# One written order for the start of a streaming-encoder kernel: a root for each row tile, the norm weight spread by one-row matmuls, queries projected beside keys and values

## The chip, the core and the metric

The kernel runs on one NeuronCore of a Trainium2 chip. Its engines work side by side, each through its own list of instructions in order: TensorE (PE in the profile; PEld is its weight load), VectorE (DVE), ScalarE (ACT), GpSimd (POOL) and SyncE (SP), which here issues the loads and most of the stores. They wait for one another by semaphores. The metric is the device time of one execution in microseconds, from three runs.

## The reference

```python
h = rmsnorm(x, norm_g)                    # x: 2048 prompt rows, then 64 sample rows, 1024 wide
q, k, v, ga, u, gb, mg = split(h @ w_in)  # w_in: 1024 x 7168
att = stick_breaking(q, k, v)             # 8 heads of 128; no softmax
pb  = multi_scale_pool(u) @ w_pool * pool_scale
m   = sigmoid(mg_a) * ((att * silu(ga)) @ w_br_a) + sigmoid(mg_b) * ((pb * silu(gb)) @ w_br_b)
y   = rmsnorm(x + m @ w_out, final_g)

def rmsnorm(x, g):
    return x * rsqrt(mean(x * x, axis=-1) + 1e-6) * g
```

Prompt and sample rows go through the same layer (the sample rows with a cache of 4096 keys and values). Keys and values are outputs too. All is fp32. A product of two matrices is made of three products of rounded fp32 halves: each operand is split into a rounded "hi" and the remainder "lo", and hi·hi, lo·hi and hi·lo are added up.

## The kernel before

**Halves and tiles.** The rows are worked in two halves: the first holds 1024 prompt rows and the 64 sample rows, nine row tiles of 128 rows (tile 8 has 64), the second the other 1024. For a half, the normalised rows are kept transposed as `hhi` and `hlo` (128 partitions, 8 blocks of the model width, all rows). From them the kernel projects slab by slab; a slab is 128 columns of `w_in`: a head's keys, values, queries or gate. `proj` (L276) loads a slab's weights in two halves of 512 columns a partition (`raw`), splits them into `whi` (ACT, L81) and `wlo` (L82, on POOL for the first head of a half), and runs 24 products for each group of rows (L284 to L286: hi·hi, lo·hi, hi·lo for 8 blocks) into a PSUM bank `pj`.

**From x to hhi.** A row tile comes as two halves of 512 columns (b = 0, 1). `square_sum` (L177) squares a half on ACT and adds it up into a column of `ss`; `root` (L87 to L93) turns the columns of several tiles at once into `rstd`, with a square root on ACT and a Newton step in tiny DVE instructions; `normalise` multiplies by `rstd` and by the norm weight `g_bc` (L204 on DVE for b = 0; for b = 1 from tile 2 on, L201 on DVE and L202 on POOL). `g_bc` are two tiles of 128 x 512 into which a DMA copies the weight for each partition (L194). `transposed_h` turns a half on PE in four transposes (L211) into a PSUM bank `tr`, of which there are two; ACT copies it to `hhi` (L81) and DVE writes the remainder to `hlo` (L82).

**The first half's start.** `prepare_x0` takes tiles 0 and 1 (loads, squares, one root, normalise), `build_h0` transposes them; then come tiles 2 and 3, 4 and 5, and 6 to 8, each set under one root. In head 0 keys and values are projected in "fine" groups of 256, 256, 256 and 320 rows, two slabs at a time, so that each group needs only two more tiles; the queries follow in groups of 512, 256 and 320, then the gate.

**The second half's start.** `build_h1` is called for tiles 0 to 3 and for 4 to 7: each time the weight is copied again by `norm_gain`, and each half tile `xb` is loaded, normalised and transposed beside the last gate slabs of the first half and the first fine slabs of the second. `g_bc` and `xb` share eight buffers (tag `be`).

**What sets the order.** PE's instructions stand as the Python code emits them; `run` interleaves generators by estimated times. The order on ACT, DVE, POOL and SP is made by the framework's scheduler, and each engine then runs its list strictly in order.

Of the kernel before, what the change touches and what calls it, by code (L numbers as in the profile page):

```python
# [11 lines left out]
ALU = mybir.AluOpType  # L12
# [32 lines left out]
def kernel(  # L45
# [4 lines left out]
    y_prompt, y_sample, k_prompt, v_prompt, pool_prompt, k_sample, v_sample, pool_sample,  # L50
):
    nc = tc.nc

    xp, xs = x_prompt[0], x_sample[0]
    yp, ys = y_prompt[0], y_sample[0]
# [20 lines left out]
    def split(hi, lo, src, eng=None):  # L76

        if eng == "v":
            nc.vector.tensor_copy(hi, src)
        else:  # L80
            nc.scalar.copy(hi, src)  # L81
        (nc.gpsimd if eng == "g" else nc.vector).tensor_tensor(lo, src, hi.bitcast(F32), op=ALU.subtract)  # L82
# [62 lines left out]
    with ExitStack() as front:  # L145
# [7 lines left out]
        def stage(name):  # L153
            return side.tile([P, 528], F32, name=name, tag="st", bufs=4)
# [27 lines left out]
        def root(c0, n):  # L182
            rsqrt_of_mean(rstd[:, c0:c0 + n], ss[:, c0:c0 + n], [t[:, c0:c0 + n] for t in sq])

        def load_x(half, i, b, t):
            src, m = row_tile(half, i)
            nc.sync.dma_start(t[0:m, 0:512], src[:, b * 512:(b + 1) * 512])
            return m

        def norm_gain():  # L190
            g = []
            for b in range(2):
                g.append(attp.tile([P, 528], F32, name="g_bc", tag="be", bufs=8))
                nc.sync.dma_start(g[b][:, 0:512], norm_g[0:1, b * 512:(b + 1) * 512].broadcast_to([P, 512]))  # L194
            return g

        def normalise(half, i, b, m, xt, gain):
            c = half * 9 + i
            x = xt[0:m, 0:512]
            if b and c > 1:  # L200
                nc.vector.tensor_scalar(x, x, rstd[0:m, c:c + 1], None, op0=ALU.mult)  # L201
                nc.gpsimd.tensor_tensor(x, x, gain[b][0:m, 0:512], op=ALU.mult)  # L202
            else:
                nc.vector.scalar_tensor_tensor(x, x, rstd[0:m, c:c + 1], gain[b][0:m, 0:512],  # L204
                                               op0=ALU.mult, op1=ALU.mult)

        def transposed_h(i, b, m, xt):
            tr = psum.tile([P, 512], F32, name="tr")
            trv = tr.rearrange("p (j r) -> p j r", j=4)
            for j in range(4):  # L210
                nc.tensor.transpose(trv[:, j, 0:m], xt[0:m, j * P:(j + 1) * P], ident[0:m, 0:m])  # L211
            split(hhi[:, b * 4:b * 4 + 4, i * P:i * P + m], hlo[:, b * 4:b * 4 + 4, i * P:i * P + m],
                  trv[:, :, 0:m])
            return 436.0

        x0 = {}
        gain0 = []

        def prepare_x0(i0, i1):
            for i in range(i0, i1):  # L220
                m = DEC if i == 8 else P
                if 4 <= i < 8:
                    both = attp.tile([P, 2, 512], F32, name="xt2", tag="v", bufs=4)
                for b in range(2):
                    if i < 4:
                        xt = attp.tile([P, 512], F32, name="xt", tag=("khi", "klo")[b], bufs=4)
                    elif i < 8:
                        xt = both[:, b]
                    else:
                        xt = stage("xt")  # L230
                    load_x(0, i, b, xt)
                    square_sum(i, b, m, xt)
                    x0[i, b] = xt
            if not gain0:
                gain0.extend(norm_gain())
            root(i0, i1 - i0)
            for i in range(i0, i1):
                for b in range(2):
                    normalise(0, i, b, DEC if i == 8 else P, x0[i, b], gain0)

        def build_h0(i0, i1):
            for i in range(i0, i1):
                for b in range(2):
                    yield transposed_h(i, b, DEC if i == 8 else P, x0[i, b])

        def stats1():
            for i in range(8):
# [13 lines left out]
                    normalise(1, i, b, P, xt, gain)  # L261
                    yield transposed_h(i, b, P, xt)

        def load_w(src, kts, width, eng=None):

            whi = pool.tile([P, kts, width], F32R, name="whi", tag="whi", bufs=2)
            wlo = pool.tile([P, kts, width], F32R, name="wlo", tag="wlo", bufs=2)
            sv = src.rearrange("(k p) c -> p k c", p=P)
            step = 512 // width
            for k in range(0, kts, step):  # L270
                raw = pool.tile([P, step, width], F32, name="raw", tag="raw", bufs=3)
                nc.sync.dma_start(raw, sv[:, k:k + step, :])
                split(whi[:, k:k + step], wlo[:, k:k + step], raw, eng)
            return whi, wlo

        def proj(groups, slabs, eng=None):  # L276


            ws = [load_w(win[:, col:col + P], KT, P, eng) for col, _ in slabs]
            for g, (c0, n) in enumerate(groups):  # L280
                for (whi, wlo), (_, evac) in zip(ws, slabs):
                    ps = psum.tile([P, 512], F32, name="pj")
                    for k in range(KT):
                        nc.tensor.matmul(ps[:, 0:n], whi[:, k], hhi[:, k, c0:c0 + n], start=k == 0, stop=False)  # L284
                        nc.tensor.matmul(ps[:, 0:n], whi[:, k], hlo[:, k, c0:c0 + n], start=False, stop=False)  # L285
                        nc.tensor.matmul(ps[:, 0:n], wlo[:, k], hhi[:, k, c0:c0 + n], start=False, stop=k == KT - 1)  # L286
# [180 lines left out]
        def head_proj(half, hd, fine=False):  # L467
# [86 lines left out]
            yield from proj(groups, [(OFF_Q + col, evac_q)])  # L554
            yield from proj(groups, [(OFF_GA + col, evac_g)])
            heads[half, hd] = out

# [281 lines left out]
        fine_ns = 2 * 24 * mm_ns(256)  # L839


        first = head_proj(0, 0, True)
# [153 lines left out]
    E = mybir.EngineType  # L996
    bpsum = ctx.enter_context(tc.tile_pool(name="bpsum", bufs=2, space=PSUM))
    ahead = {}

# [430 lines left out]
```

## Time and profile before

| | us |
|---|---|
| median of 3 runs | 2761.02 (2757.12 to 2761.07) |
| the profiled execution | 2762.22 |
| its span, first to last instruction | 2760.5 |
| granted PE clock, mean | 0.996 |
| ACT busy | 1267.9 (46%) |
| POOL busy | 583.5 (21%) |
| bytes moved by DMA | 343.87 MB, 125 GB/s |

How to read it: a row of the timeline has the start, the duration, the engine, the line of the kernel, the instruction and its tiles (`out<-in`), and in square brackets how long the engine had been idle and what ended that. A row of the waits has the waiting instruction, what ended the wait, the total in us, the number of waits and the longest. A row of the groups has the count, the busy time in us and the mean in ns. A matmul's record is longer than the distance to the next one, since matmuls are pipelined; the distance is what counts.

### The profile page before, as it was taken

The numbers are of one execution on the slowest core, as the hardware profiler recorded it, in microseconds if no ns is written. First come the engines' busy times: TensorE is split into PE (matmuls) and PEld (weight loads), VectorE is DVE, ScalarE is ACT, GpSimd is POOL, SyncE is SP. The second block draws the span as 40 slices with busy tenths as digits, with TensorE's granted clock in tenths as the row PEclk, the third lists the DMA queues.
The fourth block names the chain that finished last, engine by engine and source line by source line (L and its number), as shares of the span: only waits on it lengthen the run. The fifth ranks groups of instructions, "written<-read, shape, count | busy, mean of one in ns | idle before, by whom it ended". The sixth has DMA issues, their size and how long they took to land.

```text
span 2760.5 us, 41803 instructions
## 1 busy us (share of the span) xinstructions
PE 2702.0 (98%) x15052; PEld 2361.2 (86%) x15052; DVE 1835.7 (66%) x2843; ACT 1267.9 (46%) x2520; POOL 583.5 (21%) x1285
## 2 busy tenths in 40 slices
PE   6999999999999999999999999999999999999998
PEld 6988888888898989888888888887778889999886
DVE  6555555567777784487888888786453236777876
ACT  4445444455555553355555655564222223333443
POOL 2112222220000001322433342342004601111001
PEclk9999999999999999999999999999999999999999
DMA  5224222224444445311111111112336757786753
GB/s 149 77 83 131 75 72 72 76 94 152 150 154 153 148 147 158 97 43 58 54 45 52 50 50 43 54 46 81 106 98 218 261 176 265 257 288 224 246 160 119
DMA packets 344397, 343.87 MB, mean 125 GB/s; under 512 B 30062, under 2 KB 286558, under 8 KB 344188
## 3 DMA queue, kind: packets, MB, share of 16 engines
q1 hardware_dynamic: 329756, 294.26, 34.2%
q0 software_dynamic: 14432, 46.93, 4.8%
q8 instruction: 118, 1.93, 0.3%
q14 instruction: 91, 0.75, 0.1%
HBM read 232.46 MB, written 108.65 MB: 124 GB/s over the span
## 4 chain that ended last, share of the span: by engine, by line
PE 85%; issue 5%; DVE 5%; DMA 2%; ACT 1%; POOL 1%; SPq 0%; POOLq 0%; DVEq 0%; ACTq 0%
PE pj L284 17%; PE pj L285 17%; PE pj L286 17%; PE tr L638 4%; PE att L655 2%; PE att L654 2%; PE att L653 2%; PE z L627 2%; PE z L626 2%; PE z L625 2%; PE x L989 2%; PE x L991 2%; PE x L993 2%; PE y L989 1%; PE y L993 1%
## 5 line engine op out<-in xcount | busy, mean ns | idle before, releaser
L284 PE MATMUL pj<-hhi,whi 128*128 128x512 f32 (+2 forms) x2608 | 945.8, 363 | 0.0
L286 PE MATMUL pj<-hhi,wlo 128*128 128x512 f32 (+2 forms) x2608 | 918.2, 352 | 0.0
L285 PE MATMUL pj<-hlo,whi 128*128 128x512 f32 (+2 forms) x2608 | 917.3, 352 | 0.1
L286 PEld LDWEIGHTS pj<-hhi,wlo 128*128 128x128 f32 x2608 | 492.2, 189 | 65.1
L284 PEld LDWEIGHTS pj<-hhi,whi 128*128 128x128 f32 x2608 | 494.7, 190 | 59.5 <-ACT hhi L81 0.2
L285 PEld LDWEIGHTS pj<-hlo,whi 128*128 128x128 f32 x2608 | 493.8, 189 | 59.1 <-DVE hlo L82 0.4
L579 DVE TENSOR_TENSOR_SCAN om<-om 128x513 f32<-128x513 f32 (+3 forms) x356 | 387.7, 1089 | 212.0 <-POOL om L561 108.5
L569 ACT ACTIVATE om<-z 128x512 f32<-128x512 f32 (+2 forms) x320 | 171.6, 536 | 322.0 <-PE z L627 272.4
L82 DVE TENSOR_TENSOR wlo<-raw,whi 128x512 fp32r<-128x512 f32 x248 | 178.2, 722 | 196.6 <-ACT whi L81 195.5
L581 POOL COPY carry<-om 128x1 f32<-128x1 f32 x356 | 78.6, 221 | 918.6 <-DVE om L579 878.1
L582 DVE TENSOR_TENSOR be<-be,om 128x512 f32<-128x512 f32 (+3 forms) x356 | 230.4, 647 | 31.5
L81 ACT CAST whi<-raw 128x512 fp32r<-128x512 f32 x256 | 158.5, 624 | 182.3 <-PE pj L285 166.5
L81 ACT CAST a<-tr 128x512 fp32r<-128x512 f32 (+2 forms) x356 | 187.9, 528 | 100.6 <-PE tr L638 89.9
L82 DVE TENSOR_TENSOR a<-tr,a 128x512 fp32r<-128x512 f32 (+2 forms) x356 | 215.6, 606 | 23.9 <-ACT a L81 21.8
L638 PE MATMUL tr<-ident,be 128*128 128x128 f32 x1088 | 175.7, 274 | 6.1 <-DVE be L582 3.7
L638 PEld LDWEIGHTS tr<-ident,be 128*128 128x128 f32 x1088 | 136.1, 140 | 44.9 <-DVE be L582 8.3
L570 ACT ACTIVATE be<-z 128x512 f32<-128x512 f32 (+2 forms) x320 | 169.9, 531 | 0.0
L653 PE MATMUL att<-a,v 128*128 128x512 f32 (+1 forms) x320 | 133.2, 416 | 0.0
L574 POOL COPY om<-carry 128x1 f32<-128x1 f32 x224 | 124.1, 554 | 2.7 <-DVE be L582 0.7
L561 POOL TENSOR_SCALAR_AFFINE_SELECT om<-om 128x128 f32<-128x128 f32 x128 | 50.6, 396 | 346.1 <-ACT om L569 346.0
L655 PE MATMUL att<-a,v 128*128 128x512 f32 (+1 forms) x320 | 118.5, 370 | 3.7 <-DVE a L82 3.3
L654 PE MATMUL att<-a,v 128*128 128x512 f32 (+1 forms) x320 | 117.4, 367 | 0.0
(316 smaller groups left out, 4677.6 us busy)
## 6 DMA issues: line engine op xcount, KB each, us to landing
raw<-in_w_in_dram SPq DMA_DIRECT2D x256, 256.0 KB, 3.1
sg<-sm_d SPq DMA_DIRECT2D x48, 352.0 KB, 6.3
kraw<-in_cache_k_dram SPq DMA_DIRECT2D x64, 256.0 KB, 3.4
vraw<-in_cache_v_dram SPq DMA_DIRECT2D x64, 256.0 KB, 2.9
sm_d<-sgm SPq DMA_DIRECT2D x48, 256.0 KB, 2.5
wraw<-tw_d SPq DMA_DIRECT2D x24, 512.0 KB, 4.3
out_dram<-nat SPq DMA_DIRECT2D x42, 256.0 KB, 2.3
r<-aT_d SPq DMA_DIRECT2D x12, 704.0 KB, 7.1
```

Of the source, the lines that this page charges most:

```text
L81: nc.scalar.copy(hi, src)
L82: (nc.gpsimd if eng == "g" else nc.vector).tensor_tensor(lo, src, hi.bitcast(F32), op=ALU.subtract)
L284: nc.tensor.matmul(ps[:, 0:n], whi[:, k], hhi[:, k, c0:c0 + n], start=k == 0, stop=False)
L285: nc.tensor.matmul(ps[:, 0:n], whi[:, k], hlo[:, k, c0:c0 + n], start=False, stop=False)
L286: nc.tensor.matmul(ps[:, 0:n], wlo[:, k], hhi[:, k, c0:c0 + n], start=False, stop=k == KT - 1)
L569: nc.scalar.activation(om[:, off:512], z[:, off:512], AF.Sigmoid, scale=-SCALE)
L579: nc.vector.tensor_tensor_scan(rev, rev, rev, 1.0, op0=ALU.mult, op1=ALU.bypass)
L582: nc.vector.tensor_tensor(be[:, off:512], be[:, off:512], om[:, off + 1:513], op=ALU.mult)
L638: nc.tensor.transpose(tr[:, i * P:(i + 1) * P], be[:, off + j * P:off + (j + 1) * P], ident)
L653: nc.tensor.matmul(self.acc[:, s], vhi[:, js], ahi[:, s], start=first, stop=False)
L654: nc.tensor.matmul(self.acc[:, s], vlo[:, js], ahi[:, s], start=False, stop=False)
L655: nc.tensor.matmul(self.acc[:, s], vhi[:, js], alo[:, s], start=False, stop=last)
```

## The change

1. **One written order.** Everything from the first load to the end of head 0's queries stands in a block in which ACT, DVE and SP run in the order of the code, as PE always does. The order: squares and root of tile 0, its normalise, squares and root of tile 1, its normalise, the transposes, the weight halves, then three groups of tiles (2, 3), (4, 5), (6, 7, 8), worked between stretches of the projection (`go(n)` emits n times 6 products).
2. **A root for each row tile** (`root(i, 1)`; tiles 7 and 8 share one).
3. **The norm weight by one-row matmuls.** `gain_row` loads the 4 KB of the weight into one partition and sets a row of ones; `norm_gain` multiplies them on PE (two plain fp32 products of 1 x 128 by 1 x 512) into the two PSUM banks `att`. `normalise` reads the weight there, always in one DVE instruction (L209 of the new file); POOL's multiplications by the weight are gone. The same holds in `build_h1`.
4. **Queries beside keys and values.** In head 0 of each half three slabs are projected in the fine groups. The queries' weights use the two buffers `a`, which the attention has no use for yet; three of the first six weight halves come into the buffers `om`.
5. **Loads** of all nine tiles and of six weight halves are issued first, in order of need.

```diff
-        def norm_gain():
+        def gain_row():
+            ones = side.tile([P, P], F32, name="ones", tag="sgs", bufs=2)
+            nc.gpsimd.memset(ones[0:1], 1.0)
+            row = attp.tile([P, 2, 512], F32, name="g_row", tag="v", bufs=4)
+            nc.sync.dma_start(row[0:1], norm_g[0:1].rearrange("o (b c) -> o b c", b=2))
+            return ones, row
+
+        def norm_gain(row=None):
+            ones, row = row or gain_row()
             g = []
             for b in range(2):
-                g.append(attp.tile([P, 528], F32, name="g_bc", tag="be", bufs=8))
-                nc.sync.dma_start(g[b][:, 0:512], norm_g[0:1, b * 512:(b + 1) * 512].broadcast_to([P, 512]))
+                g.append(psum.tile([P, 512], F32, name="att"))
+                nc.tensor.matmul(g[b], ones[0:1], row[0:1, b], start=True, stop=True)
             return g
...
-            if b and c > 1:
-                nc.vector.tensor_scalar(x, x, rstd[0:m, c:c + 1], None, op0=ALU.mult)
-                nc.gpsimd.tensor_tensor(x, x, gain[b][0:m, 0:512], op=ALU.mult)
-            else:
-                nc.vector.scalar_tensor_tensor(x, x, rstd[0:m, c:c + 1], gain[b][0:m, 0:512],
-                                               op0=ALU.mult, op1=ALU.mult)
+            nc.vector.scalar_tensor_tensor(x, x, rstd[0:m, c:c + 1], gain[b][0:m, 0:512],
+                                           op0=ALU.mult, op1=ALU.mult)
...
             if fine:
-                yield from proj(FINE_B if half else FINE_A, [(OFF_K + col, evac_k), (OFF_V + col, evac_v)], "g")
+                yield from proj(FINE_B if half else FINE_A,
+                                [(OFF_K + col, evac_k), (OFF_V + col, evac_v), (OFF_Q + col, evac_q)], "g", ws)
...
-        prepare_x0(0, 2)
-        run((build_h0(0, 2), 1.0))
-        run((take(first, 1.0), 1.0))
-        for i0, i1 in ((2, 4), (4, 6), (6, 9)):
-            prepare_x0(i0, i1)
-        for i0, i1 in ((2, 4), (4, 6), (6, 9)):
-            run((take(first, fine_ns - 1000), fine_ns), (build_h0(i0, i1), 4 * 436.0))
-        constants()
+        with tc.manual_schedule(engines={E.Activation, E.DVE, E.SP}):
...
+            for i in range(2):
+                squares_x0(i)
+                root(i, 1)
+                if i == 0:
+                    normalise_x0(0)
+            normalise_x0(1)
...
+            for g, tiles in enumerate(((2, 3), (4, 5), (6, 7, 8))):
+                squares_x0(tiles[0])
+                if g == 1:
+                    constants()
+                go(3)
+                root(tiles[0], 1)
+                go(1)
+                if g == 0:
+                    for k in (0, 4):
+                        split0(2, k)
+                normalise_x0(tiles[0])
+                for i in tiles[1:]:
+                    squares_x0(i)
+                root(tiles[1], len(tiles) - 1)
+                go(4)
+                for i in tiles[1:]:
+                    normalise_x0(i)
+                go(2)
+                turn_x0(tiles[0])
+                go(2)
+                for i in tiles[1:]:
+                    turn_x0(i)
+            run((take(first, 72 * mm_ns(320) - 1.0), 1.0))
```

How the lists change at the places that matter. First DVE's list from the program's start: `ss` are the sums of squares, `sq` and `rstd` the steps of the root, L204 the normalise of half a tile. Before:

```order
L180 TENSOR_TENSOR ss<-ss,acc 128x1 x2
L87 TENSOR_SCALAR sq_95<-ss 128x2
L89 RECIPROCAL rstd<-sq_96 128x2
L90 TENSOR_TENSOR sq_96<-rstd 128x2
L91 TENSOR_TENSOR sq_96<-sq_96,sq_95 128x2
L92 TENSOR_SCALAR sq_96<-sq_96 128x2
L93 TENSOR_TENSOR rstd<-rstd,sq_96 128x2
L409 CAST identr<-ident 128x128
L415 COPY ident_89<-ident 64x64
L416 COPY ident_89<-ident 64x64
L204 SCALAR_TENSOR_TENSOR xt<-xt,rstd,g_bc 128x512 x4
```

And after, where `att` is the bank with the weight and L209 the normalise:

```order
L181 TENSOR_TENSOR ss<-ss,acc 128x1
L88 TENSOR_SCALAR sq_95<-ss 128x1
L90 RECIPROCAL rstd<-sq_96 128x1
L91 TENSOR_TENSOR sq_96<-rstd 128x1
L92 TENSOR_TENSOR sq_96<-sq_96,sq_95 128x1
L93 TENSOR_SCALAR sq_96<-sq_96 128x1
L94 TENSOR_TENSOR rstd<-rstd,sq_96 128x1
L209 SCALAR_TENSOR_TENSOR xt<-xt,rstd,att 128x512 x2
L181 TENSOR_TENSOR ss<-ss,acc 128x1
L88 TENSOR_SCALAR sq_95<-ss 128x1
L90 RECIPROCAL rstd<-sq_96 128x1
```

The root now serves one tile, its two normalises follow at once, and the next tile's root stands behind them; the constants have moved into the second group.

Next DVE's list in the change's group of tiles 2 and 3, from the end copy of the first keys (`khi`, `klo`) to the remainders of the second tile:

```order
L80 CAST khi<-kst 128x256
L83 TENSOR_TENSOR klo<-kst,khi 128x256
L209 SCALAR_TENSOR_TENSOR xt<-xt,rstd,att 128x512 x2
L181 TENSOR_TENSOR ss<-ss,acc 128x1
L88 TENSOR_SCALAR sq_95<-ss 128x1
L90 RECIPROCAL rstd<-sq_96 128x1
L91 TENSOR_TENSOR sq_96<-rstd 128x1
L92 TENSOR_TENSOR sq_96<-sq_96,sq_95 128x1
L93 TENSOR_SCALAR sq_96<-sq_96 128x1
L94 TENSOR_TENSOR rstd<-rstd,sq_96 128x1
L209 SCALAR_TENSOR_TENSOR xt<-xt,rstd,att 128x512 x2
L889 TENSOR_TENSOR hlo<-tr,hhi 128x4x128 x2
```

Both tiles' normalises now stand ahead of the first tile's `hlo`, and the second tile's `hlo` behind that.

Last SP's list at the start of the second half: `xb` are its half tiles, `sm_d<-sgm` the stores of the last gate slabs, `raw` the weight halves. Before:

```order
L194 DMA g_bc<-in_norm_g_dram 128x512 x2
L187 DMA xb<-in_x_prompt_dram 128x512 x4
L306 DMA sm_d<-sgm 128x320
L272 DMA raw<-in_w_in_dram 128x4x128
L187 DMA xb<-in_x_prompt_dram 128x512
L272 DMA raw<-in_w_in_dram 128x4x128
```

and further down, for the second set of tiles:

```order
L187 DMA xb<-in_x_prompt_dram 128x512 x2
L306 DMA sm_d<-sgm 128x256
L194 DMA g_bc<-in_norm_g_dram 128x512 x2
L187 DMA xb<-in_x_prompt_dram 128x512 x2
L306 DMA sm_d<-sgm 128x256
```

After, at the same two places:

```order
L188 DMA xb<-in_x_prompt_dram 128x512 x6
L321 DMA sm_d<-sgm 128x320
L276 DMA raw<-in_w_in_dram 128x4x128
L188 DMA xb<-in_x_prompt_dram 128x512
L276 DMA raw<-in_w_in_dram 128x4x128
```
```order
L321 DMA sm_d<-sgm 128x512 x2
L188 DMA xb<-in_x_prompt_dram 128x512 x2
L321 DMA sm_d<-sgm 128x256
L188 DMA xb<-in_x_prompt_dram 128x512 x2
L321 DMA sm_d<-sgm 128x256
```

The weight's copies no longer stand ahead of the rows, and the second set's first rows are issued one store earlier.

More of the change, by code (lines that the diff above doesn't have):

```diff
@@ L52 @@
     nc = tc.nc
+    E = mybir.EngineType
     xp, xs = x_prompt[0], x_sample[0]
@@ L211, in transposed_h, with block_h @@
                 nc.tensor.transpose(trv[:, j, 0:m], xt[0:m, j * P:(j + 1) * P], ident[0:m, 0:m])
-            split(hhi[:, b * 4:b * 4 + 4, i * P:i * P + m], hlo[:, b * 4:b * 4 + 4, i * P:i * P + m],
-                  trv[:, :, 0:m])
+            return trv[:, :, 0:m]
+        def block_h(t, i, b, m):
+            return t[:, b * 4:b * 4 + 4, i * P:i * P + m]
+        def transposed_h(i, b, m, xt):
+            split(block_h(hhi, i, b, m), block_h(hlo, i, b, m), turned_h(m, xt))
             return 436.0
@@ L217, with rows0, fetch_x0, squares_x0 @@
         gain0 = []
[L219 to L244, printed above, removed]
+        def rows0(i):
+            return DEC if i == 8 else P
+        def fetch_x0(i, bs=(0, 1)):
+            for b in bs:
+                if i < 4:
+                    xt = attp.tile([P, 512], F32, name="xt", tag=("khi", "klo")[b], bufs=4)
+                elif i < 6:
+                    xt = attp.tile([P, 512], F32, name="xt", tag=("kraw", "vraw")[b], bufs=2)
+                else:
+                    if b == 0:
+                        x0[i] = attp.tile([P, 2, 512], F32, name="xt2", tag="v", bufs=4)
+                    xt = x0[i][:, b]
+                load_x(0, i, b, xt)
+                x0[i, b] = xt
+        def squares_x0(i):
+            for b in range(2):
+                square_sum(i, b, rows0(i), x0[i, b])
+        def normalise_x0(i):
+            for b in range(2):
+                normalise(0, i, b, rows0(i), x0[i, b], gain0)
         def stats1():
@@ L262, in build_h1, with raw_w, form_w, load_w @@
                     yield transposed_h(i, b, P, xt)
[L264 to L273, printed above, removed]
+        def raw_w(col, k, spare=False):
+            if spare:
+                raw = attp.tile([P, 513], F32, name="raws", tag="om", bufs=3)[:, 0:512].rearrange("p (k c) -> p k c", k=4)
+            else:
+                raw = pool.tile([P, 4, P], F32, name="raw", tag="raw", bufs=3)
+            nc.sync.dma_start(raw, win[:, col:col + P].rearrange("(k p) c -> p k c", p=P)[:, k:k + 4, :])
+            return raw
+        def form_w(spare=False):
+            if spare:
+                return [attp.tile([P, KT, P], F32R, name=nm, tag="a", bufs=2) for nm in ("wqhi", "wqlo")]
+            return [pool.tile([P, KT, P], F32R, name=nm, tag=nm, bufs=2) for nm in ("whi", "wlo")]
+        def load_w(col, eng=None, spare=False):
+            whi, wlo = form_w(spare)
+            for k in range(0, KT, 4):
+                split(whi[:, k:k + 4], wlo[:, k:k + 4], raw_w(col, k), eng)
             return whi, wlo
-        def proj(groups, slabs, eng=None):
-            ws = [load_w(win[:, col:col + P], KT, P, eng) for col, _ in slabs]
+        def proj(groups, slabs, eng=None, ws=()):
+            ws = list(ws) + [load_w(col, eng, n == 2) for n, (col, _) in enumerate(slabs) if n >= len(ws)]
             for g, (c0, n) in enumerate(groups):
@@ L465, in natural, with head_proj @@
             return nat
-        def head_proj(half, hd, fine=False):
+        def head_proj(half, hd, fine=False, ws=()):
             groups = groups_of(half)
@@ L553, in head_proj @@
                 yield from proj(groups, [(OFF_V + col, evac_v)])
-            yield from proj(groups, [(OFF_Q + col, evac_q)])
+                yield from proj(groups, [(OFF_Q + col, evac_q)])
             yield from proj(groups, [(OFF_GA + col, evac_g)])
@@ L837, in heads_phase @@
             return chain(att.steps(H - 1), att.steps(None)), att.head_ns(H - 1) + 6000.0
[L839 to L850 removed]
+        fine_ns = 3 * 24 * mm_ns(256)
```

52 lines of the change are left out of this document (49 added, 3 removed).

## The prediction

> **What bounds the kernel now.** I read first the busy times, then who waits for whom on TensorE (PE), then the stretches of the span in which PE waits.
>
> ```profile
> PE 2702.0 (98%) x15052; PEld 2361.2 (86%) x15052; DVE 1835.7 (66%) x2843; ACT 1267.9 (46%) x2520; POOL 583.5 (21%) x1285
> ```
> ```profile
> PE tr L211 <- DVE xt L204: 15.1, 2, 14.2
> PE tr L211 <- DVE hlo L82: 4.9, 3, 3.3
> PE tr L211 <- DVE rstd L89: 3.1, 1, 3.1
> ```
>
> PE is busy for 98% of the span, so only what PE waits for, or runs slowly, can be won. Its longest waits all end at L211, the transposes of x: once at the very start (14.2 us) and several times behind VectorE (DVE) rows. The stretches show where:
>
> ```profile
> core 0: us, PE busy (x) PEld busy (x) DVE busy (x) ACT busy (x) POOL busy (x), PEclk, DMA share, GB/s
> 0.00:10.00 10.00, 0.00 (x0) 0.00 (x0) 1.63 (x6) 5.71 (x14) 1.99 (x8) 1.00 0.80 240
> 10.00:20.00 10.00, 4.91 (x18) 3.52 (x19) 8.37 (x17) 5.27 (x13) 4.90 (x23) 1.00 0.88 297
> 20.00:30.00 10.00, 9.15 (x54) 8.88 (x54) 9.29 (x26) 7.97 (x27) 3.25 (x3) 1.00 0.74 146
> 30.00:40.00 10.00, 6.34 (x40) 5.93 (x40) 9.24 (x19) 2.98 (x7) 4.60 (x4) 0.83 0.20 66
> 40.00:50.00 10.00, 9.02 (x78) 8.75 (x77) 7.22 (x12) 4.44 (x9) 3.08 (x3) 1.00 0.18 54
> 50.00:60.00 10.00, 8.99 (x71) 8.40 (x69) 3.40 (x8) 3.42 (x9) 0.00 (x0) 1.00 0.22 66
> 1110.00:1115.00 5.00, 1.77 (x16) 1.56 (x13) 2.84 (x4) 1.87 (x4) 2.67 (x3) 1.00 0.89 276
> 1115.00:1120.00 5.00, 4.90 (x29) 4.90 (x30) 3.41 (x8) 1.24 (x3) 2.07 (x2) 0.66 0.27 90
> ```
>
> PE is idle for 60 less 38.4, or 21.6 us of the first 60, and 3.2 us at 1110. The change touches these two places and no others: outside them each engine's instructions stand in the same order in both programs. So I work out two things: when the first score product of head 0 starts (PE's order up to there holds the same work in both), and what the start of the second half loses.
>
> **The first place, before.** How the start is spent:
>
> ```profile
> 3.60 0.63 ACT L177 ACTIVATE jk<-xt 128x512 f32<-128x512 f32 x1 [1.28 <-DMA xt<-in_x_prompt_dram]
> 6.50 0.63 ACT L177 ACTIVATE jk<-xt 128x512 f32<-128x512 f32 x1 [1.57 <-DMA xt<-in_x_prompt_dram]
> 8.85 3.71 POOL L82 TENSOR_TENSOR wlo<-raw,whi 128x512 fp32r<-128x512 f32 x3 [7.36 <-ACT whi L81]
> 9.10 1.02 DVE L90 TENSOR_TENSOR sq<-rstd 128x2 f32<-128x2 f32 x1
> 11.38 1.20 DVE L92 TENSOR_SCALAR sq<-sq 128x2 f32<-128x2 f32 x1
> 13.32 2.74 DVE L204 SCALAR_TENSOR_TENSOR xt<-xt,rstd,g_bc 128x512 f32<-128x512 f32 x4
> 19.66 0.58 PE L285 MATMUL pj<-hlo,whi 128*128 128x256 f32 x1
> 88.09 0.22 PE L625 MATMUL z<-khi,qhi 128*128 128x128 f32 x1
> ```
>
> The root serves two tiles at once, so it waits for tile 1's loads; then three of its tiny steps take 1.0 to 1.2 us each, because each ends only with one of GpSimd's (POOL) 1.24 us subtractions. PE's projection runs on from 19.66, and the first score product comes at 88.09. The same root without POOL beside it:
>
> ```profile
> 20.63 0.16 DVE L180 TENSOR_TENSOR ss<-ss,acc 128x1 f32<-128x1 f32 x1
> 22.33 0.75 DVE L204 SCALAR_TENSOR_TENSOR xt<-xt,rstd,g_bc 128x512 f32<-128x512 f32 x1
> ```
>
> 1.7 us from the sum of the squares to the normalise.
>
> **The first place, after: the start.** Tile 0's second half is now third in the load queue, behind the 4 KB weight row. I put it at 4.7 (bounds 4.2 and 6.5: when the second and the third load had landed). Its square and the accumulator's read add 0.8: 5.5. One root: 7.2. Two normalises (pitch 2.74/4 = 0.68): 8.7. Tile 1's root stands behind them on DVE: 10.4. Two normalises: 11.8. Tile 1's transposes on a slow PE take 1.1 and the copy to hhi 0.6; DVE's first hlo of tile 1 then ends at **13.6**, where the projection can run on. That is 6.1 us earlier than 19.66. The weight halves hide behind this: ScalarE's (ACT) copy at 10.6, POOL's 1.24 from 11.3.
>
> The weight spread needs two plain fp32 products on PE before the normalises. No row shows one of 512 columns. The nearest:
>
> ```profile
> 847.67 0.43 PE L802 MATMUL tr<-ident,as 128*128 128x64 f32 x2 [0.36 <-DVE as L796]
> 847.95 0.28 PE L718 MATMUL tr<-ident,kraw 128*128 128x128 f32 x1
> 46.06 0.44 PE tr L211 x4
> ```
>
> L802 is one plain fp32 product of 64 columns, recorded as two and over in 0.28 us; four fp32 transposes of 128 columns take 0.44, 0.86 ns a column. Two records of 512 columns at that rate: 0.88 us, which I take, since the columns and not the weight load fill such a product. Low end: two at the 0.23 us of a rounded 512-column product, 0.46. High end: 0.28 times 8, 2.2. At the slow clock 0.88 doubles; with the row landing near 4.0 the two are done by 5.8 and 7.6, before their normalises at 7.2 and 7.9: free. At the high end the second is done at 12.8 and the start slips by about 4.5.
>
> **The first place, after: the run.** PE's pitch per product:
>
> ```profile
> 20.25 0.41 PE L284 MATMUL pj<-hhi,whi 128*128 128x256 f32 x1
> 20.47 0.41 PE L285 MATMUL pj<-hlo,whi 128*128 128x256 f32 x1
> 28.42 0.28 PE L284 MATMUL pj<-hhi,whi 128*128 128x256 f32 x1
> 28.54 0.28 PE L285 MATMUL pj<-hlo,whi 128*128 128x256 f32 x1
> 87.64 0.31 PE L284 MATMUL pj<-hhi,whi 128*128 128x320 f32 x1
> 87.79 0.31 PE L285 MATMUL pj<-hlo,whi 128*128 128x320 f32 x1
> 92.31 0.39 PE L285 MATMUL pj<-hlo,whi 128*128 128x512 f32 x1
> 92.54 0.39 PE L286 MATMUL pj<-hhi,wlo 128*128 128x512 f32 x1
> ```
>
> 0.118 us for 256 columns (0.21 until PE has run warm), 0.147 for 320, 0.23 for 512. Keys, values and queries in three groups of 256: 216 x 0.118 = 25.5. All four slabs' 320: 96 x 0.147 = 14.1. The gate slab's others: 24 x 0.23 + 24 x 0.118 = 8.4. Transposes of tiles 2 to 8: 14 x 0.44 = 6.2; of keys and values: 18 x 0.11 = 2.0. Sum 56.2. That queries now run in 256s costs nothing: two at 0.118 against one at 0.23.
>
> Slow clock: PE took from 19.66 to about 26.7 to leave the 0.21 pitch, with a gap between; unbroken work leaves it sooner. I take 3 us of half speed: 1.5 lost (bounds 0.8 and 3.4).
>
> Waits: in each later group of tiles DVE's list is the longer one. Its durations:
>
> ```profile
> L204 DVE SCALAR_TENSOR_TENSOR xt<-xt,rstd,g_bc 128x512 f32<-128x512 f32 x10 | 7.2, 749 | 0.1
> L82 DVE TENSOR_TENSOR hlo<-tr,hhi 128x512 fp32r<-128x512 f32 x16 | 10.9, 685 | 4.9 <-ACT hhi L81 4.7
> L82 DVE TENSOR_TENSOR klo<-kst,khi 128x256 fp32r<-128x256 f32 x4 | 1.7, 415 | 0.1
> ```
>
> Two roots at 1.7, four normalises at 0.68, four hlo at 0.64, keys 0.72, values 0.72, qlo 0.43: 10.5 us; 9.8 in the first group, which has no values yet, 11.6 in the second, where the masks stand in between, and 12.9 in the last, which has three tiles. PE's list against it: 8.5, 8.5 and 9.4 us (54 products, 6.4, and the transposes). The next keys wait for the group's last hlo, so PE waits the differences, 1.3, 3.1 and 3.5, and 1.4 more in the last, where six transposes pass through two banks that hlo frees: 9.3 in all. The gain operand now comes from a PSUM bank; hlo reads PSUM too and is no slower for it, so I keep 0.68. Each 0.1 more costs about 2.3 us over the three groups.
>
> 13.6 + 56.2 + 1.5 + 9.3 = **80.6, or 7.5 us before 88.09.** From 19.66 the same sum for before (56.2, 4.8 of slow clock, 6.5 of waits) ends at 87.2, 0.9 short; so it is good to about a microsecond.
>
> **The second place.**
>
> ```profile
> 1113.96 0.49 DVE L201 TENSOR_SCALAR xb<-xb,rstd 128x512 f32<-128x512 f32 x1 [0.98 <-DMA xb<-in_x_prompt_dram]
> 1115.10 0.66 PE L211 MATMUL tr<-ident,xb 128*128 128x128 f32 x4 [3.33 <-DVE hlo L82]
> ```
>
> The wait is a late load: the 512-column copies of the weight hold two of the eight buffers that x comes into and stand in the queue ahead of it. After, x has all eight, its loads stand ahead of the others, and POOL multiplies nothing. So 3.3 goes, and the slow clock behind it (0.66 over 4.9 us: 1.7). Added on PE, uncovered: four fp32 products, 4 x 0.88 = 3.5, and 0.2 twice until the first normalise behind them. Net 5.0 - 3.9 = **1.1 won** (bounds: 2.8 won, 4.4 lost). The third slab's weight halves are late only if POOL's six take over 9 us; they take 7.6.
>
> Together 8.6. The profiled execution took 2762.2 (span 2760.5 and 1.7 around it), 1.2 above the median of 2761.0; 2762.2 - 8.6 = 2753.6, and for the median **2752.4**.
>
> **A rule weighed.** After an idle 3.11 us PE's pitch fell back to 0.21 (granted clock 0.83 in 30 to 40), and after 3.33 again (0.66). My longest single wait is some 3.0 us, in the last group. The Trainium skill, page "TensorE: Matmul & The Clock Gate", section "Part 1: The HAM clock gate", says that the clock halves after an idle window of about 3.4 us that runs free of the program. By that rule a wait of 3.0 need not fill a window; the two rows above fell at less than 3.4, so the trace is a little harsher than the rule.
>
> **Rivals.**
> - *The clock falls in the last group's wait.* Price 1.7 us as at 1115: 2754.1. Still faster. For it: 3.11 was enough once.
> - *DVE eats the early start.* Were a normalise from PSUM 0.2 us longer, waits grow by 4.6 and the gain is 4.0: 2757, within 0.2%. Against: the hlo row.
> - *Slower: the hand order couples the roots to POOL.* Should six tiny steps of each group's two roots take 1.0 us as at 9.10, 4.8 us a group go to DVE, which PE waits for, 14.4 in all: 2767. It decides where POOL works through all three groups; its row is empty of tile work once the third slab's halves are done near 22, so only the first group can be touched, for 1 us.
> - *The change doesn't do what it says:* fp32 products at 2.2 us put back 4.5 at the start and 5.5 at 1110: 2762, no change.
>
> **How the numbers follow.** Forecast 0.55, clock 0.20, DVE 0.13, slow products 0.05, slower 0.04, and 0.03 for a start as good with fewer waits (2748). Within 0.2% is what a measurement can tell from nothing, 5.5 us. Faster by more: 0.55 + 0.20 + 0.03 = 0.78; same 0.13 + 0.05 = 0.18; slower 0.04. The range: 1.3 us of start, 2 of clock, 2 of waits, and the second place's bounds: 2747 to 2757.5.
>
> **What would show it.** The first normalise near 7.3 and the projection running on near 13.6; three waits of PE near 2, 3 and 5 us before the key slabs, each ended by hlo; the first score product near 80.6; no wait of 3 us near 1110, and fp32 records of 0.4 to 0.5 us pitch. It is wrong if DVE's normalise is longer than 0.75, or if weight halves or loads, and not DVE, end PE's waits.

## The result, and the profile after

| | before | after |
|---|---|---|
| median of 4 runs, us | 2760.39 (2757.12 to 2761.07) | 2746.03 (2741.77 to 2746.59) |
| ratio after to before | | 0.9945, 95% interval 0.9933 to 0.9956 |
| span of the profiled execution | 2760.5 | 2744.9 |

The time fell by 14.4 us, or 15.6 between the two profiled executions. The forecast was 8.6. First the page's busy times after, then who PE waits for up to 90 us (releaser; total, number, longest).

```profile
PE 2700.3 (98%) x15136; PEld 2368.1 (86%) x15136; DVE 1831.3 (67%) x2866; ACT 1268.5 (46%) x2527; POOL 567.0 (21%) x1277
```
```profile
PE att L203 <- DMA g_row<-in_norm_g_dram: 3.6, 1, 3.6
PE tr L474 <- DVE hlo L889: 3.4, 3, 2.2
PE tr L216 <- DVE hlo L889: 1.0, 4, 0.5
PE z L216 <- DVE xt L209: 0.9, 1, 0.9
PE tr L216 <- DVE xt L209: 0.8, 1, 0.8
PE pj L300 <- DVE hlo L889: 0.7, 2, 0.3
```

The long waits for roots and loads are gone, and those for `hlo` are what was expected in kind. The timeline of the same execution, at the places that the prediction names:

```profile
3.60 3.75 PE L203 MATMUL att<-g_row,ones 1*128 1x512 f32 x4 [3.60 <-DMA g_row<-in_norm_g_dram]
7.27 1.41 DVE L209 SCALAR_TENSOR_TENSOR xt<-xt,rstd,att 128x512 f32<-128x512 f32 x2
13.49 0.58 PE L300 MATMUL pj<-hlo,whi 128*128 128x256 f32 x1
38.38 0.44 PE L474 MATMUL tr<-ident,kst 128*128 128x128 f32 x2 [0.70 <-DVE hlo L889]
54.53 0.57 PE L474 MATMUL tr<-ident,kst 128*128 128x128 f32 x2 [2.17 <-DVE hlo L889]
57.65 0.69 PE L216 MATMUL tr<-ident,xt 64*128 64x64 f32 x4 [0.55 <-DVE hlo L889]
85.22 0.22 PE L641 MATMUL z<-khi,qhi 128*128 128x128 f32 x1
1086.34 1.98 PE L203 MATMUL att<-g_row,ones 1*128 1x512 f32 x4
1159.70 0.22 PE L641 MATMUL z<-khi,qhi 128*128 128x128 f32 x1
```

The start is as forecast: first normalise at 7.27, projection running on at 13.49. But the first score product comes at 85.22, only 2.9 us earlier than before, not 7.5. The stretches show why (the third number from the end of a row is the granted clock):

```profile
30.00:40.00 10.00, 9.14 (x76) 8.54 (x74) 7.48 (x24) 4.68 (x14) 0.00 (x0) 1.00 0.20 66
40.00:50.00 10.00, 9.42 (x64) 9.14 (x64) 5.28 (x18) 5.36 (x18) 0.00 (x0) 0.83 0.27 80
50.00:60.00 10.00, 7.09 (x42) 5.82 (x41) 7.25 (x16) 4.13 (x10) 0.00 (x0) 0.74 0.05 13
60.00:70.00 10.00, 10.00 (x56) 9.96 (x55) 2.79 (x8) 2.63 (x6) 0.00 (x0) 0.75 0.25 76
1085.00:1090.00 5.00, 5.00 (x25) 3.45 (x24) 2.45 (x4) 1.18 (x2) 0.00 (x0) 0.89 0.14 53
1090.00:1095.00 5.00, 5.00 (x35) 5.00 (x35) 3.68 (x7) 1.56 (x3) 0.00 (x0) 0.76 0.42 133
1110.00:1115.00 5.00, 5.00 (x33) 5.00 (x32) 3.90 (x8) 1.58 (x3) 1.28 (x1) 0.72 0.57 161
```

PE's clock falls in the first groups, and again from 1085 on, where PE does not idle at all. So the two places that the change touches gave little. To find where the time came from instead, I cut the span at three instructions of PE: the first score product of each half (the `z` rows above) and the first product of the output phase (`x<-rhi,b11hi`, at 2256.47 before and 2243.32 after).

| us | up to the first score product | from there to the second half's | from there to the output phase | from there to the end | span |
|---|---|---|---|---|---|
| before | 88.09 | 1074.63 | 1093.75 | 504.03 | 2760.5 |
| after | 85.22 | 1074.48 | 1083.62 | 501.58 | 2744.9 |

Ten of the 15.6 us come from the third stretch, in which every instruction stands in the same order in both programs. There is no wait in it that went: PE idles for 8.0 us of it before and 8.2 after. (Of the 2.5 us in the last stretch, up to 1.7 are a fall of the clock from 2600.8 to 2604.2 in the profile before, which the one after does not have.) Here is a piece of it that holds gate projections and nothing else on PE, first before, then after:

```profile
2100.00:2200.00 100.00, 100.00 (x431) 80.44 (x430) 25.80 (x22) 23.04 (x41) 63.47 (x81) 1.00 0.78 253
```
```profile
2100.00:2200.00 100.00, 100.00 (x443) 82.78 (x442) 25.13 (x22) 24.23 (x42) 65.73 (x81) 1.00 0.83 268
```

PE is busy for all 100 us at full clock in both, yet does 443 products of 512 columns where it did 431. Measured from start to start over some 750 of them, the pace is 0.2335 us before and 0.2270 after.

### The profile page after: what moved, and what is told of

It reads as the page before. It is cut to its first block, busy times and chain, and to the rows that moved or that the text cites. A ratio compares the mean times of both kernels' runs of the same rounds, so it can differ in the third digit from the quotient of the medians.

```text
span 2744.9 us, 41961 instructions
## 1 busy us (share of the span) xinstructions
PE 2700.3 (98%) x15136; PEld 2368.1 (86%) x15136; DVE 1831.3 (67%) x2866; ACT 1268.5 (46%) x2527; POOL 567.0 (21%) x1277
## 4 chain that ended last, share of the span: by engine, by line
PE 89%; DVE 5%; DMA 2%; issue 2%; ACT 1%; POOL 0%; SPq 0%; DVEq 0%; POOLq 0%; ACTq 0%
PE pj L299 17%; PE pj L300 17%; PE pj L301 17%; PE tr L654 4%; PE x L1083 3%; PE x L1085 3%; PE x L1087 3%; PE att L671 2%; PE att L670 2%; PE att L669 2%; PE z L643 2%; PE z L642 2%; PE z L641 2%; PE y L1083 2%; PE y L1085 2%; PE y L1087 2%
## 5 line engine op out<-in xcount | busy, mean ns | idle before, releaser
L299 PE MATMUL pj<-hhi,whi 128*128 128x512 f32 (+2 forms) x2568 | 929.7, 362 | 0.5 <-ACT hhi L886 0.5
L301 PE MATMUL pj<-hhi,wlo 128*128 128x512 f32 (+2 forms) x2568 | 902.7, 352 | 0.0
L300 PE MATMUL pj<-hlo,whi 128*128 128x512 f32 (+2 forms) x2568 | 901.9, 351 | 0.8 <-DVE hlo L889 0.7
L669 PE MATMUL att<-a,v 128*128 128x512 f32 (+1 forms) x320 | 132.6, 414 | 0.0
L671 PE MATMUL att<-a,v 128*128 128x512 f32 (+1 forms) x320 | 118.6, 371 | 3.7 <-DVE a L83 3.4
L643 PE MATMUL z<-khi,qlo 128*128 128x512 f32 (+2 forms) x320 | 116.8, 365 | 0.0
```

Of the source, the lines that this page charges most:

```text
L643: nc.tensor.matmul(z[:, off:512], qlo[:, qs], khi[:, 0:m], start=False, stop=True)
L669: nc.tensor.matmul(self.acc[:, s], vhi[:, js], ahi[:, s], start=first, stop=False)
L671: nc.tensor.matmul(self.acc[:, s], vhi[:, js], alo[:, s], start=False, stop=last)
```

## Experiments

**What differs in that stretch?** Not the order. But the tiles' addresses do: `acc` (four small columns) used to be the first buffer allocated behind `hlo`, and now comes after `whi`, `wlo` and `raw`, since the first squares are now emitted later than the first weight buffers. So `whi` and `wlo` moved by 128 bytes in every partition, from 87680 to 87552, which is a multiple of 512, as are the beginnings of `hhi` (17920) and `hlo` (52736). These addresses are worked out from the allocations; the traces hold none. Two kernels exchange just that (`acc` and `raw` move along). `b_aligned` is the kernel before with

```diff
         hlo = pool.tile([P, KT, RA], F32R, name="hlo")
+        pool.tile([P, KT, P], F32R, name="whi", tag="whi", bufs=2)
+        pool.tile([P, KT, P], F32R, name="wlo", tag="wlo", bufs=2)
+        pool.tile([P, 4, P], F32, name="raw", tag="raw", bufs=3)
```

> The kernel before, with one thing changed: the buffers whi and wlo are allocated ahead of acc, so that they begin at a multiple of 512 bytes of each partition (87552) and not 128 bytes behind one (87680), as they do in the changed kernel. Instructions and their order are those of before. Theory P (the placement of the weights sets the pace of the 512-column products: 0.2331 us in the long gate stretch of before, 0.2269 after): the pace falls to 0.227, some 1500 such products give 8 to 10 us there and a few more elsewhere, and the time is 2746 to 2751; the start keeps its first score product at 88.1. Theory O (the order of the change won it all, and the pace is a matter of chance or of the surroundings): 2758 to 2762, pace 0.233.

and `a_shifted` is the changed kernel with

```diff
         hlo = pool.tile([P, KT, RA], F32R, name="hlo")
+        pool.tile([P, 1], F32, name="acc", tag="acc", bufs=4)
```

> The changed kernel, with acc allocated first, so that whi and wlo stand at 87680 as in before; instructions and order are those of the changed kernel. Theory P: the pace goes back to 0.233 and the time to 2757 to 2761, within 0.2 percent of before: the written order alone is worth 0 to 3 us. Theory O: it stays at 2744 to 2748.

Measured: `b_aligned` 2748.98 us (2745.43 to 2750.85), ratio to before 0.9957 (0.9945 to 0.9970); `a_shifted` 2757.42 (2754.01 to 2760.70), ratio 0.9991 (0.9982 to 1.0). The same 100 us, in `b_aligned` and then in `a_shifted`:

```profile
2100.00:2200.00 100.00, 100.00 (x443) 82.84 (x442) 26.15 (x22) 24.09 (x42) 65.77 (x81) 1.00 0.82 266
```
```profile
2100.00:2200.00 100.00, 100.00 (x430) 80.42 (x430) 22.47 (x24) 22.70 (x39) 61.56 (x77) 1.00 0.81 257
```

The pace goes with the address and not with the order. The placement alone wins 10.9 us on the kernel before; the written order alone wins 2.4 us, which its interval hardly tells from nothing; together 13.3 of the 14.4. Theory P stands.

**Is it the address itself or a distance?** Four versions of the changed kernel, run once each: `a_all128` (128 unused bytes ahead of `hhi`, so that all four move), `a_256` and `a_64` (256 and 64 unused bytes behind `hlo`, so that only the weights move) and `a_wlo128` (only `wlo` moves).

```diff
+        pool.tile([P, 32], F32, name="pad")     # a_all128
         hhi = pool.tile([P, KT, RA], F32R, name="hhi")
         hlo = pool.tile([P, KT, RA], F32R, name="hlo")
+        pool.tile([P, 64], F32, name="pad")     # a_256; [P, 16] in a_64
+        pool.tile([P, KT, P], F32R, name="whi", tag="whi", bufs=2)   # a_wlo128
+        pool.tile([P, 1], F32, name="acc", tag="acc", bufs=4)        # a_wlo128
```

> The changed kernel with 128 unused bytes ahead of hhi, so that hhi, hlo, whi and wlo all stand 128 bytes further on and keep their distances from each other. If what counts is where the weights stand against hhi and hlo (two reads that collide), the pace in the gate stretch stays at 0.227 us and the span near 2744; if it is the place of the weights by itself (128 bytes off a multiple of 512), the pace is 0.233 and the span 2754 to 2757.

> The changed kernel with whi and wlo 256 bytes further on, hhi and hlo as they are. If any offset from a multiple of 512 bytes costs as much: pace 0.233, span 2754 to 2757. If a multiple of 256 is enough: 0.227, span near 2744. Anything between would say that the cost grows with the offset.

> The changed kernel with only wlo 128 bytes further on (whi stays at 87552). If each product pays for its own weights, the mean pace lies between: of three products one has wlo, so 0.229 where all three off gave 0.233 and none gave 0.227; span 2747 to 2749. If one buffer off spoils all three: 0.233.

> The changed kernel with whi and wlo 64 bytes further on, hhi and hlo as they are. At a distance of 0 or 256 bytes (beyond a multiple of 512) the pace was 0.227, at 128 0.2335. If two reads collide whenever they are not in step within 256 bytes, 64 gives 0.2335 too; if only the half period does, 0.227; a value between would say that it grows with the distance.

| | whi, wlo moved against hhi, hlo by | pace, us | span, us |
|---|---|---|---|
| after | 0 | 0.2270 | 2744.9 |
| a_all128 | 0 (all moved by 128) | 0.2271 | 2747.0 |
| a_256 | 256 | 0.2270 | 2745.6 |
| a_wlo128 | 0 and 128 | 0.2314 | 2749.9 |
| a_64 | 64 | 0.2336 | 2753.9 |
| a_shifted | 128 | 0.2335 | 2754.3 |

The row of `a_all128`, the one that decides:

```profile
2100.00:2200.00 100.00, 100.00 (x443) 82.81 (x442) 26.46 (x22) 23.42 (x40) 63.80 (x80) 1.00 0.81 264
```

It is a distance: weights 128 bytes off a multiple of 512 are as fast as any if the moving rows are off by as much. 64 costs as much as 128. Steps of 256 bytes cost nothing, but `a_256` alone does not show that: the blocks of `hhi` and `hlo` are 4352 bytes apart, 17 times 256, and those of the weights 512, so in every version half of the products stand 256 bytes (beyond multiples of 512) further off than the other half, and `a_256` only exchanges the halves. What shows it is that inside the changed kernel both halves keep the same pace (0.2267 us at the even and at the odd ones of blocks 4 to 7).

With `wlo` alone displaced, two thirds of the loss appear and not the one third expected. By product, the distance to the next one is 0.2276 us for hi·hi, 0.2325 for lo·hi and 0.2340 for hi·lo: slow are the product that uses `wlo` and the one before it, during which `wlo` is loaded. So a product does not simply pay for its own weights; which two reads hinder each other stays open.

**Why did the first place give 2.9 and not 7.5?** `a_warm` adds products that nobody reads, 29 of 256 columns, in the groups of tiles 4, 5 and 6 to 8 of the changed kernel; `a_turns` has as many transposes of `ident` in their place.

```diff
+            def busy(n):
+                z = psum.tile([P, 512], F32, name="z")
+                for _ in range(n):
+                    nc.tensor.matmul(z[:, 0:256], ws[0][0][:, 0], hhi[:, 0, 0:256], start=True, stop=True)
...
                 turn_x0(tiles[0])
-                go(2)
+                go(1)
+                if g:
+                    busy(6 * g)
+                go(1)
                 for i in tiles[1:]:
                     turn_x0(i)
+                    if g:
+                        busy(5 if g == 1 else 3)
```

> The changed kernel with products added whose result nothing reads: in the groups of tiles 4, 5 and 6 to 8, 11 and 18 products of 256 columns (0.118 us each, 3.4 in all) among the transposes and ahead of the waits for the key slabs. Theory C (transposes count as no work for the clock, so a stretch of waits and transposes of 3 to 4 us halves it): the clock stays at 1.0 from 40 to 66, which gives back up to 6 us (1.7 of the stretch at 41, 4.5 of the one at 54 to 65), most of the added products lie in waits, and the first score product comes at 80 to 83 instead of 85.2; the time is 2 to 5 us less. Theory W (the clock falls by the waits alone, whatever fills the rest): the clock falls as before, and the time is the same or up to 3 us longer.

> The changed kernel with 29 transposes of 128 columns added at the places where the other version had products of 256 columns (0.11 us each, 3.2 in all), in the groups of tiles 4, 5 and 6 to 8. If transposes count as no work for the clock, it falls as in the changed kernel, at the latest before the last group's key slab (0.5 for 7 to 10 us from about 54), and the first score product comes at 82 to 86. If any busy PE keeps the clock, it stays at 1.0 from 20 to 80 as with the added products, and the first score product comes at 79 to 81.

Measured: `a_warm` 2744.03 us (2742.44 to 2745.14), ratio to before 0.9940 (0.9926 to 0.9953), first score product at 79.86; `a_turns`, run once, 2742.39, first score product at 81.17. The clock in `a_warm`, then in `a_turns`:

```profile
40.00:50.00 10.00, 9.75 (x83) 9.59 (x82) 6.74 (x25) 6.19 (x20) 0.00 (x0) 1.00 0.22 67
50.00:60.00 10.00, 8.37 (x64) 7.52 (x63) 6.13 (x12) 2.94 (x7) 0.00 (x0) 1.00 0.13 39
60.00:70.00 10.00, 10.00 (x65) 9.55 (x64) 3.68 (x7) 4.04 (x10) 0.00 (x0) 1.00 0.45 131
```
```profile
50.00:60.00 10.00, 8.20 (x66) 7.31 (x65) 7.13 (x15) 3.79 (x9) 0.00 (x0) 1.00 0.05 15
60.00:70.00 10.00, 10.00 (x68) 9.81 (x67) 3.99 (x8) 3.76 (x9) 0.00 (x0) 1.00 0.50 147
```

With 3.4 us more work the same stretch ends 5.4 us sooner than in the changed kernel's profile, because the clock stays up. Products and, in the one execution of `a_turns`, transposes both do it, so my theory C, that transposes count as no work, falls. What seems to count is how much of a few microseconds PE waits: 2.9 of the last group's 10 without the additions (7.09 busy), 1.6 with (8.37). The time of `a_warm` itself cannot be told from the changed kernel's: their intervals overlap.

The fall is also a matter of chance. Eight profiled executions ran these groups with nothing added: in the last group the clock fell in all eight, near 41 us in four of them, and the first score product came between 81.81 and 85.27. The changed kernel's own profile, at 85.22, is at the slow end, so the additions are worth 2 to 5.4 us here.

The traces show what the chance is. In all 14 profiles the granted clock changes only at points whose distances are multiples of 3.413 us (to within 0.03), up to PE's last instruction; where these points lie differs from one execution to the next. Four such intervals of the changed kernel, then one of `a_turns` in which PE has nothing but transposes:

```profile
37.64:41.06 3.42, 1.98 (x13) 1.26 (x12) 2.38 (x6) 2.13 (x5) 0.00 (x0) 1.00 0.21 61
41.06:44.47 3.41, 3.41 (x16) 3.41 (x17) 0.69 (x2) 0.92 (x4) 0.00 (x0) 0.50 0.27 79
51.30:54.71 3.41, 1.24 (x12) 1.04 (x10) 3.41 (x6) 0.69 (x2) 0.00 (x0) 1.00 0.00 0
54.71:58.12 3.41, 2.83 (x14) 2.07 (x13) 1.75 (x4) 1.54 (x3) 0.00 (x0) 0.50 0.13 38
```
```profile
54.22:57.64 3.42, 2.50 (x21) 2.06 (x22) 2.02 (x5) 1.94 (x5) 0.00 (x0) 1.00 0.13 38
```

Over all 14 profiles, and leaving aside the intervals with one-row products (below), the clock fell at the end of all 19 full-clock intervals in which PE was busy for less than 0.45 of the time, of 6 of the 24 with 0.45 to 0.64, and of none of some 11,000 with more. Four of those six are the falls near 41 us, in intervals (0.58 to 0.63) that are mostly transposes; so a transpose may count for less than a product, but the last row (2.50 of 3.42 us, no fall) shows that it counts.

**Why did the second place win nothing?** `a_copies` brings the weight for the second half by two copies, made once, into two buffers that are idle there; `a_fullrow` keeps the products on PE but over 128 rows, of which 127 of `row` are zero.

```diff
+        gain1 = []
+
         def build_h1(i0, i1):
-            gain = norm_gain()
+            if not gain1:                        # a_copies
+                for b in range(2):
+                    gain1.append(attp.tile([P, 512], F32, name="g_bc", tag="kraw", bufs=2))
+                    nc.sync.dma_start(gain1[b], norm_g[0:1, b * 512:(b + 1) * 512].broadcast_to([P, 512]))
+            gain = gain1
```
```diff
-            gain = norm_gain()
...
+            nc.gpsimd.memset(ones, 1.0)          # a_fullrow
...
+            nc.gpsimd.memset(row, 0.0)
+            nc.sync.dma_start(row[0:1], norm_g[0:1].rearrange("o (b c) -> o b c", b=2))
...
+                nc.tensor.matmul(gain[b], ones, row[:, b], start=True, stop=True)
```

> The changed kernel, but at the start of the second half the norm weight comes by two DMA copies, made once, into the two buffers kraw, which nothing uses there; its eight buffers be stay free for x. The four fp32 one-row products (two stretches of 1.96 us) go, and with them, if the low pace behind each (0.21 for 256 columns from 1089.1 to 1092.2 and from 1109.4 to 1112.7) is theirs, some 3 us of slow clock. Theory C (a stretch of one-row products and transposes lets the clock fall although PE is busy): 3.9 + 3 = 6 to 7 us less, 2739 to 2740, no slow stretch between 1085 and 1115. Theory N (the slow stretches have another cause): 3 to 4 us less, 2742 to 2743, slow stretches stay. If the copies land late, a wait of 3 us comes back near 1090 and the gain is nil.

> The changed kernel, but in the second half the products that spread the norm weight use all 128 rows (ones, times a tile that is zero except for the weight in row 0): the same number of instructions and columns, the same result. If the clock falls there because a one-row product counts as almost no work, it stays at 1.0 from 1085 to 1115 (the changed kernel and the one with shifted weights show three slow stretches there in two runs), and the second half's first score product comes 1071 us behind the first one, not 1074.5. If plain fp32 products count for nothing whatever their rows, one or two stretches of 3.2 us at the 0.21 pitch stay.

Measured: `a_copies` 2742.01 us (2741.02 to 2743.28), ratio to before 0.9934 (0.9921 to 0.9946); `a_fullrow`, run once, 2742.09. From the first score product of one half to that of the other: 1074.48 after, 1067.87 in `a_copies`, 1071.60 in `a_fullrow`. First `a_copies`, then `a_fullrow`:

```profile
1085.00:1090.00 5.00, 5.00 (x45) 5.00 (x44) 2.41 (x5) 2.15 (x4) 0.00 (x0) 1.00 0.49 153
1090.00:1095.00 5.00, 5.00 (x38) 4.98 (x38) 4.25 (x7) 2.17 (x5) 0.00 (x0) 1.00 0.54 169
```
```profile
1085.00:1090.00 5.00, 5.00 (x38) 4.19 (x37) 4.88 (x8) 1.56 (x3) 0.00 (x0) 1.00 0.40 127
1090.00:1095.00 5.00, 5.00 (x42) 4.99 (x41) 3.22 (x6) 2.15 (x4) 0.00 (x0) 1.00 0.61 191
1110.00:1115.00 5.00, 5.00 (x46) 5.00 (x45) 3.72 (x7) 2.14 (x5) 0.00 (x0) 1.00 0.18 52
```
```profile
1084.02 1.88 PE L271 MATMUL att<-g_row,ones 128*128 128x512 f32 x4
```

With copies 6.6 us go from this stretch, as theory C asked for here: the products and the slow clock. The time came to 2742.0 and not to the 2739 to 2740 expected: in the profiled execution the two later stretches took 5.2 us more than in the changed kernel's (1085.75 and 504.69, against 1083.62 and 501.58), with a fall of the clock in each of them (at 1159.0 and 2254.7) that the changed kernel's profile does not have. Only a first score product at 81.81, earlier by chance, made up for 3.4 of it.

With full rows the products take nearly as long (1.88 us for two), and the clock does not fall: 2.9 us back. The single row is therefore the likely cause of the slow stretch behind each pair, but on little evidence. In the eight profiled executions that have one-row products there the clock fell behind 13 of 16 pairs: behind 13 of the 14 that lie within one interval of 3.413 us, and behind neither of the two that an interval's end divides. (Counted as idle, a whole pair leaves PE busy for 0.45 of its interval.) Of the two pairs of `a_fullrow`, in its single execution, one is divided in this way too, so only the other (at 1102.21) speaks. In the four versions of the changed kernel without one-row products the clock never fell there.

**Both edits together, and the keys' distance.** `a_copies_warm` joins `a_copies` and `a_warm`. `a_best` adds to that 64 unused bytes ahead of `mask2`, which moves the keys against the queries.

```diff
+        side.tile([P, 16], F32, name="pad")
         mask2 = side.tile([P, DEC], F32R, name="mask2")
```

> The changed kernel with both earlier edits: the second half's norm weight by two copies into kraw (2742.0 alone) and the 29 added products in the first half's groups (2744.0 alone). If the two gains lie at places of their own, they add up: 4.0 + 2.0 under 2746.0, so 2740; the first score product at 80, the second half's 1068 later, near 1148. If the first edit had won only by a lucky turn of the clock in the first groups, 2742 to 2744.

> The version with copies and added products (2743.0), with 64 unused bytes ahead of mask2, which move all of attp by 64: the moving keys khi and klo now stand at a distance of 0 (modulo 256 bytes) from the stationary queries, where they stood at 192. If the distance matters in the score products as it does in the projections, their 512-column pace falls by up to 0.006 us, for some 1700 full-size products 2 to 6 us less: 2737 to 2741. If it matters only where PE has nothing but projections, 2742 to 2744.

Measured: `a_copies_warm` 2742.96 us (2741.17 to 2744.30), ratio to before 0.9938 (0.9924 to 0.9951), first score product at 80.02 and 1068.58 from there to the second half's; `a_best` 2742.91 (2742.23 to 2746.68), ratio 0.9941 (0.9927 to 0.9955). At both places the gains add up as expected, and yet the time is not below that of `a_copies`. Some is given back later: from the first product of the output phase to the end it takes 505.3 us where the changed kernel took 501.6, and part of it shows as a wait there that the changed kernel does not have:

```profile
2251.41 0.43 PE L1099 MATMUL x<-rhi,t2hi 128*128 128x352 f32 x1 [1.75 <-ACT rhi L82]
```

Most of the rest is a fall of the clock right behind this wait, which costs up to 1.7 us and which the changed kernel's profile does not have there:

```profile
2254.36:2257.78 3.42, 3.42 (x14) 3.42 (x13) 3.35 (x5) 0.00 (x0) 0.73 (x1) 0.50 0.86 252
```

For the keys, the expectation failed: the score products' pace did not fall (0.234 mean in `a_best`, 0.232 in `a_copies_warm`). The distance is shown to matter for the projections alone. Of all these, `a_copies` has the lowest median, 4 us under the changed kernel; its interval overlaps that kernel's.

## Why the prediction was wrong

**The step that failed** is "The change touches these two places and no others: outside them each engine's instructions stand in the same order in both programs." The sentence about the order is true and the conclusion is not: the change also moved `whi` and `wlo`, and the pitch of 0.23 us for a 512-column product, which I took from before and held fixed, became 0.227 in the unbroken runs of projections. That is 10.9 us, alone more than the whole forecast, and none of my rivals or bounds held it. The sign was right, but mostly for a reason that I did not give: the two places that I did price, together 8.6, gave 2.4 (the written order alone, from `a_shifted`).

Step by step:
- **The start** was right: 13.6 forecast, 13.49 measured, and DVE's normalise (743 ns mean, from PSUM) no longer than before.
- **fp32 products**: 0.88 forecast, 0.98 measured (1.96 us for two, from 1086.34 to the transposes at 1088.30); 1.88 each at the start's slow clock, where they lay in front of the normalise and cost nothing, as forecast.
- **Waits before the key slabs**: 9.3 forecast, 5.6 measured (1.26, 1.44 and 2.88 for the three groups), ended by `hlo` as forecast but for 0.24 in each of the first two, which `hhi` ended; the second and third were priced too high.
- **Slow clock**: 1.5 forecast, bounds 0.8 to 3.4. The pitch of the products above its warm value, summed from 12.7 to the first score product, comes to 8.1 us after and to 3.2 in `a_warm`. This is the mis-sized term of the first place: 6.6 us more than forecast, against 3.7 that the waits gave back. The transposes ran at the slow clock too, which the sum did not hold: less the waits they take 10.3 us, where the sum had 8.2 and `a_warm` has 8.2. With these figures the sum comes out: 13.5, 48.0 for the products, 8.1, 10.3 and 5.6 make 85.5 (measured 85.22); for `a_warm` 13.4, 48.0, 3.2, 8.2, 3.4 added and 3.4 of waits make 79.6 (measured 79.86). The rival of a falling clock was there (0.20), priced at 1.7 us from a wait of 3; it came with a wait of 2.17 and stayed for ten microseconds, after a first fall of 3.4 us near 41.
- **The second place**: 1.1 won was forecast; 0.15 was measured (1074.63 before, 1074.48 after). The wait of 3.3 went and the products cost 3.9, both as forecast; the slow clock of 1.7 did not go but came twice, behind products that keep PE busy by the profile. How much the old order costs here varies: `b_aligned`, which has it at the new pace, took 1071.27, in part because the clock did not fall behind its wait of 2.39. At the old pace `a_64` took 1074.52 and `a_shifted` 1075.86.
- **A price that decided nothing**: 0.1 us more for a normalise was put at 2.3 us over the three groups; their 14 normalises make 1.4. The rival that DVE eats the early start was priced too high by this.
- **The rule weighed.** The Trainium skill, page "TensorE: Matmul & The Clock Gate", section "Part 1: The HAM clock gate", lets the clock fall after an idle window of about 3.4 us. Its free-running window of that length agrees with the points 3.413 us apart and with the four falls in eight near 41 us. Its "idle" does not agree with the falls at 54.71, behind an interval in which PE was busy for 1.24 of 3.41 us and waited 2.17 at the longest, nor with the falls at 1089 and 1109, where the profile shows PE busy without a gap.

## What to carry to other kernels

An unchanged order is not an unchanged program: after any edit that adds, drops or delays an allocation, compare the buffers' addresses, and look at the pace of the commonest product in a stretch that the edit should not touch. Where products run back to back, try the weights at a distance from the moving rows that is a multiple of 256 bytes. And price PE's waits with the clock that they cost, which can be more than the wait; a few products thrown into a stretch full of waits can be better than free for what follows (first score product at 79.86, against 81.81 to 85.27).

## What the runs showed of the hardware

- The pace of unbroken 512-column products hangs on the distance between stationary and moving operand in a partition: 0.2270 us at 0 or 256 bytes (beyond multiples of 512), 0.2335 at 64 or 128. Where products are mixed with other work (100 to 1080 us) the projections show a quarter of the difference (0.2358 after and 0.2359 in `b_aligned`, 0.2375 before and in `a_shifted`), and the score products none that goes with it.
- The granted clock changes only at points 3.413 us apart, whose place differs from execution to execution. One-row products aside, it fell behind all 19 such intervals with PE busy for less than 0.45 and behind none of some 11,000 with PE busy for more than 0.64.
- One-row fp32 products make PE busy in the profile, but the clock falls behind them (granted clock down to 0.72 over five microseconds; 13 of 14 pairs that lie within one interval). With 128 rows, mostly zeros, it did not fall behind the one pair that can be compared.
- Identity transposes hold the clock up too: an interval with 2.50 of 3.42 us of them and no product ended without a fall.
- The same instructions can come 3.4 us earlier or later by where the clock's falls land: the first score product at 85.22 in the changed kernel, at 81.81 in `a_copies`, which has the same instructions up to there.
